# Adding the experts' output rows in DRAM by accumulating scatters, with the final norm beside the last expert, in a two-layer decoder trunk

## The chip, the cores and the metric

The kernel is one program on one core of a Trainium2 chip. The metric is the device time of one execution in microseconds (us). A core has the engines TensorE (PE in the profile, with PEld for its weight loads), VectorE (DVE), ScalarE (ACT), GpSimd (POOL) and SyncE (SP), and 16 DMA engines that all queues share.

## The reference, cut to what matters

512 tokens of width 1024 pass two layers. Layer 0 mixes tokens by a gated MLP and memory attention, layer 1 by dilated attention and memory attention. After each mixer comes a layer norm, and then a mixture of 16 experts of which each token uses two:

```python
x = layer_norm(ALPHA * x + att, ln1_g[layer], ln1_b[layer])
h = x.reshape(B * S, D)
expert, gate = route(h, w_router, b_router)          # two experts a token
ffn = moe_ffn(h, expert, gate, w_gate[layer], w_up[layer], w_down[layer])
x = layer_norm(ALPHA * x + ffn, ln2_g[layer], ln2_b[layer])
# in moe_ffn, for each expert's block of 128 rows:
return (jax.nn.silu(xblk @ w_gate[e]) * (xblk @ w_up[e])) @ w_down[e]
```

All arrays are float32.

## The kernel before, in words

`trunk` (L1422) runs `layer_a`, `moe(0)`, `layer_b`, `moe(1)` and a last block that ends layer 1.

**Experts.** `stream` (L1193) goes through the 16 experts one after the other. An expert has one block of 128 slots; a token that uses it has a rank among its tokens, and that is its slot (1024 slots are used over 16 experts, 64 of 128 in the mean). Its weights (12.6 MB) come as six halves of 2 MB through a ring of eight 2 MB slots (`load_half`, L1092): as soon as half n is used up, half n+8 is loaded into its place by SP. `block` (L1134) works in 24 chunks c of two matmuls by 128x512: c 0-3 and 4-7 are the first halves of gate and up, 8-11 and 12-15 the second halves, 16-19 and 20-23 the two halves of the down product. To keep float32 precision with fast matmuls, each weight chunk is split into a high and a low part in float32r: ACT copies the high part four chunks ahead, DVE subtracts the low part three chunks ahead (`get`, L1253; the profile's `wh` and `wl`), and `products` (L1125) makes three matmuls of each one (`mm3`, L121). The engines PE, ACT and DVE take their instructions in the order in which the program writes them (`InOrder`, L59); `jobs` hangs small work at the end of a chunk: the slot-to-token index of expert e+2, the gather of its rows (`gather`, L1075, an indirect DMA of POOL from `hbuf`), the transposes of the next rows.

**Adding up.** ACT copies the down product out of PSUM into a tile `y`, and `scatter` (L1080, an indirect DMA of POOL) writes its rows to `ybuf`, which has two rows for each token, so that no row is written twice; the scatters are declared free of each other, and unused slots are skipped because their index lies beyond the bounds. `ybuf` starts as zeros: POOL writes them in `layer_a` (L352, five DMAs of 1 MB with the copy `zbuf`), and `layer_b` writes them again for layer 1 (L555). `hbuf` holds the experts' input rows; `store` (L813) writes it after the first norm, tile by tile.

**The end of a layer.** While the last expert runs, `tail_slot` (L1290) loads the second norm's weights, reads two pairs of 128-token tiles from `hbuf` (SP), and adds the two rows of `ybuf` to each with accumulating DMAs of POOL (L1311). The last expert's rows are not scattered: a one-hot matrix `oT` brings them to their tokens by matmuls (`last_slots`, L1313). `combine` (L1384) then does, for each of the four tiles, identity matmul plus one-hot matmuls into PSUM (`z`), statistics on DVE, the normalising copy on ACT; in layer 1 `rest` (L1432) multiplies and adds the norm's weights on POOL or DVE and stores the tile by SP.

**Index.** `rows` (L1055) turns the sums of a small matmul into two indices, for `hbuf` and for `ybuf`.

## Time and profile before

| | us |
|---|---|
| median of 3 runs (1672.14 to 1672.54) | 1672.16 |
| the profiled execution, its own time | 1676.11 |
| its span, first to last instruction | 1674.4 |
| busy in the span: PE / DVE / ACT / POOL | 1582.7 / 1388.4 / 1130.7 / 181.6 |
| moved by DMA | 496.39 MB |

The profile is of one execution. Its starts are in us from the span's start. The profiled execution lies 3.95 us above the median of the runs, of which 1.7 us are outside the span.

### The profile page before, as it was taken

To read this page: it belongs to the slowest core of one execution; us is meant where nothing else is said; L and a number is where in the kernel's file an instruction comes from. 1 tells how busy PE (TensorE), PEld (TensorE's weight loads), DVE (VectorE), ACT (ScalarE), POOL (GpSimd) and SP (SyncE) were. 2 spreads that over 40 slices of the span, in tenths; PEclk is the share of its full clock that TensorE was granted. 3 is DMA by queue.
4 is the path that set the end of the run, shared out by engine and by line. 5 is a ranking of instruction groups with operands and counts; after the bars stand their busy time and mean duration, and the time that the engine had idled before them with its cause. 6 is when DMAs were issued, how large, how long until landed. Compare 5 with 4: busy or idle time off the path is not lost. (4 is left out here: it accounts for less than half of the span.)

```text
span 1674.4 us, 21460 instructions
## 1 busy us (share of the span) xinstructions
PE 1582.7 (95%) x7608; PEld 1278.8 (76%) x7608; DVE 1388.4 (83%) x1936; ACT 1130.7 (68%) x1443; POOL 181.6 (11%) x149
## 2 busy tenths in 40 slices
PE   7999889999999999999699998599999999999995
PEld 5778668888888888887587786488888888888883
DVE  3856789999999999997735556799999999999997
ACT  3544458888888888886324434288888888888882
POOL 1201400000000000001400000200000000000012
PEclk9999979999999999999799997699999999999998
DMA  8516579999999999988631151699999999999974
GB/s 347 220 51 252 202 283 378 362 380 381 370 377 365 383 380 378 373 339 243 239 123 57 64 227 32 226 362 378 379 371 365 380 373 381 380 367 381 376 233 101
DMA packets 53125, 496.39 MB, mean 296 GB/s; under 512 B 10117, under 2 KB 10245, under 8 KB 24272
## 3 DMA queue, kind: packets, MB, share of 16 engines
q1 hardware_dynamic: 39344, 449.44, 68.9%
q0 software_dynamic: 13088, 43.39, 8.1%
q10 hardware_dynamic: 576, 2.10, 0.3%
q8 instruction: 62, 1.02, 0.2%
q14 instruction: 55, 0.45, 0.1%
HBM read 479.86 MB, written 34.64 MB: 307 GB/s over the span
## 5 line engine op out<-in xcount | busy, mean ns | idle before, releaser
L68 DVE TENSOR_TENSOR wl<-wexp,wh 128x1024 fp32r<-128x1024 f32 x768 | 918.4, 1220 | 43.3 <-ACT wh L68 8.9
L68 ACT ACTIVATE wh<-wexp 128x1024 fp32r<-128x1024 f32 x762 | 797.6, 1059 | 133.7 <-PE pg L68 58.7
L68 PE MATMUL pd<-wh,ah 128*128 128x512 f32 x512 | 209.6, 409 | 0.0
L68 PE MATMUL pg<-wh,xh 128*128 128x512 f32 x512 | 204.6, 400 | 1.3 <-ACT xh L68 1.3
L68 PE MATMUL pd<-wl,ah 128*128 128x512 f32 x512 | 202.7, 396 | 0.0
L68 PE MATMUL pu<-wh,xh 128*128 128x512 f32 x512 | 202.4, 395 | 0.0
L68 PE MATMUL pd<-wh,al 128*128 128x512 f32 x512 | 202.1, 395 | 0.0
L68 PE MATMUL pg<-wl,xh 128*128 128x512 f32 x512 | 200.9, 392 | 0.0
L68 PE MATMUL pg<-wh,xl 128*128 128x512 f32 x512 | 200.8, 392 | 0.0
L68 PE MATMUL pu<-wl,xh 128*128 128x512 f32 x512 | 199.7, 390 | 0.0
L68 PE MATMUL pu<-wh,xl 128*128 128x512 f32 x512 | 199.2, 389 | 0.0
L68 PEld LDWEIGHTS pd<-wl,ah 128*128 128x128 f32 x512 | 96.1, 188 | 22.9
L68 PEld LDWEIGHTS pg<-wl,xh 128*128 128x128 f32 x512 | 96.9, 189 | 21.0
L68 PEld LDWEIGHTS pg<-wh,xh 128*128 128x128 f32 x512 | 96.9, 189 | 20.9 <-ACT xh L68 1.9
L68 PEld LDWEIGHTS pg<-wh,xl 128*128 128x128 f32 x512 | 97.1, 190 | 20.2 <-DVE xl L68 0.9
L68 PEld LDWEIGHTS pd<-wh,al 128*128 128x128 f32 x512 | 96.5, 188 | 20.0 <-DVE al L68 0.4
L68 PEld LDWEIGHTS pu<-wl,xh 128*128 128x128 f32 x512 | 96.1, 188 | 20.4
L68 PEld LDWEIGHTS pd<-wh,ah 128*128 128x128 f32 x512 | 96.3, 188 | 18.9
L68 PEld LDWEIGHTS pu<-wh,xl 128*128 128x128 f32 x512 | 96.2, 188 | 19.0
L68 PEld LDWEIGHTS pu<-wh,xh 128*128 128x128 f32 x512 | 96.1, 188 | 18.8
L1077 POOL DMA_INDIRECT xg<-hbuf,ix x32 | 42.0, 1312 | 580.5 <-PE pu L68 467.1
L1081 POOL DMA_INDIRECT ybuf<-y,ix x30 | 38.6, 1285 | 449.4 <-ACT y L68 449.4
(369 smaller groups left out, 2248.1 us busy)
## 6 DMA issues: line engine op xcount, KB each, us to landing
wexp<-w_moe SPq DMA_DIRECT2D x177, 2048.0 KB, 9.1
wexp<-w_moe SPq DMA_DIRECT2D x24, 1024.0 KB, 8.0
yrows<-ybuf POOLq DMA_DIRECT2D x8, 1024.0 KB, 9.8
wb<-wbr SPq DMA_DIRECT2D x4, 2048.0 KB, 10.6
wexp<-w_moe POOLq DMA_DIRECT2D x3, 2048.0 KB, 10.5
ybuf<-mematt POOLq DMA_DIRECT2D x4, 1024.0 KB, 14.3
wina<-wina SPq DMA_DIRECT2D x2, 2048.0 KB, 19.3
wouta<-w_out_a SPq DMA_DIRECT2D x2, 2048.0 KB, 10.9
```

The source lines that it names most:

```text
L68: r = getattr(self.eng, name)(*args, **kw)
L1077: return self.nc.gpsimd.indirect_dma_start(out=xg, out_offset=None, in_=self.hbuf, in_offset=off, bounds_check=S - 1, oob_is_err=False)
L1081: st = self.nc.gpsimd.indirect_dma_start(out=self.ybuf, out_offset=bass.IndirectOffsetOnAxis(ap=ix[:, 1], axis=0), in_=y, in_offset=None, ...
```

## The change

One DRAM buffer `sbuf` of 512 + 128 rows takes the place of `ybuf` and `zbuf`. `store` writes the norm's rows to `hbuf` and to `sbuf`; each scatter adds its 128 rows to `sbuf` in DRAM (`compute_op=OP.add`), unused slots to the 128 spare rows. The scatters are no longer declared free of each other. Layer 0 still ends in `combine`, reading `sbuf` in place of `hbuf` and `ybuf`. In layer 1 `combine` goes away. Beside the last expert, all 512 rows of `sbuf` are loaded, normalised by DVE and written by `put`, an indirect DMA by token index, whose index skips the tokens that the last expert works on; those are gathered in slot order, get the down product added, are normalised and written by one more `put`. The down product of that expert is one float32 matmul on the unsplit weights in place of three float32r ones. The gather of the first two experts now skips unused slots.

```diff
-        self.ybuf = tc.dram_tile([2 * S, D], F32, name="ybuf")
+        self.sbuf = tc.dram_tile([S + P, D], F32, name="sbuf")
         self.xbuf = tc.dram_tile([S, D], F32, name="xbuf")
-        self.zbuf = tc.dram_tile([2 * P, D], F32, name="zbuf")
...
-            for rows in [self.ybuf[2 * t * P:2 * (t + 1) * P] for t in range(NT)] + [self.zbuf]:
-                nc.gpsimd.dma_start(rows.rearrange("(p k) d -> p (k d)", k=2), zero)
+            nc.gpsimd.dma_start(self.sbuf[S:], zero[:, :D])
...
-            for t in range(NT):
-                nc.gpsimd.dma_start(self.ybuf[2 * t * P:2 * (t + 1) * P], self.zbuf)
...
-        def store(t):
-            nc.sync.dma_start(self.hbuf[t * P:(t + 1) * P, :], xr[:, t])
+        def store(*tiles):
+
+            for buf in (self.hbuf, self.sbuf):
+                for t in tiles:
+                    nc.sync.dma_start(buf[t * P:(t + 1) * P, :], xr[:, t])
...
         def between():
             for t in late:
                 rows(t)
-                store(t)
+            store(*late)
...
-        nc.vector.tensor_scalar(self.info[:, :, :, 0], o12[:, :, 1], self.p2, None, op0=OP.add)
...
-        self.dve.tensor_scalar(ix[:, 1], f, float(SKIP), None, op0=OP.add)
-        if mask:
-            return self.dve.tensor_scalar(ix[:, 0], ix[:, 1], 1, mask, op0=OP.arith_shift_right, op1=OP.bitwise_and)
-        return self.dve.tensor_scalar(ix[:, 0], ix[:, 1], 1, None, op0=OP.arith_shift_right)
+        return self.dve.tensor_scalar(ix, f, float(SKIP), self.free, op0=OP.add, op1=OP.min)
...
-    def scatter(self, y, ix, nodep):
-        st = self.nc.gpsimd.indirect_dma_start(out=self.ybuf, out_offset=bass.IndirectOffsetOnAxis(ap=ix[:, 1], axis=0),
-                                               in_=y, in_offset=None, bounds_check=2 * S - 1, oob_is_err=False)
-        for other in nodep:
-            self.tc.declare_no_dep(st.ins, other.ins, reason="rows of other tokens")
-        nodep.append(st)
+    def scatter(self, y, ix):
+
+        self.nc.gpsimd.indirect_dma_start(out=self.sbuf, out_offset=bass.IndirectOffsetOnAxis(ap=ix, axis=0),
+                                          in_=y, in_offset=None, bounds_check=S + P - 1, compute_op=OP.add)
...
-        self.dve.tensor_sub(parts[1][:, s], x3, parts[0][:, s].bitcast(F32))
+        if len(parts) > 1:
+            self.dve.tensor_sub(parts[1][:, s], x3, parts[0][:, s].bitcast(F32))
...
-        h, l = part
         for q in range(2):
             kt = 2 * j + q
             c = slice(q * 512, (q + 1) * 512)
+            if len(a) == 1:
+                self.pe.matmul(bank, a[0][:, kt], part[:, c], start=(kt == 0), stop=(kt == 7))
+                continue
+            h, l = part
             self.mm3(bank, (a[0][:, kt], a[1][:, kt]), (h[:, c], l[:, c]), start=(kt == 0), stop=(kt == 7),
                      order=((0, 0), (1, 0), (0, 1)))
...
+        final = layer == 1
+        split = 24 * NE - 8 * final
...
+            elif not final:
+                spread((11, 12, 13), self.last_slots(pool))
             else:
-                spread((11, 12, 13), self.last_slots(pool))
+                whole = [self.y_tile().rearrange("p (k n) -> p k n", k=KT)]
+                bg = self.norm_rest(pool)
+                do(0, lambda: next(bg))
+                for s in range(12, 24):
+                    do(s, lambda: next(bg, None))
...
-                while len(his) < min(k + AHEAD_H + 1, 24 * NE):
+                while len(his) < min(k + AHEAD_H + 1, split):
                     his.append(self.wh_tile())
                     self.hi = self.act.activation(his[-1], chunk(len(his) - 1), AF.Copy)
-                while len(los) < min(k + AHEAD_L + 1, 24 * NE):
+                while len(los) < min(k + AHEAD_L + 1, split):
                     n = len(los)
                     los.append(self.wl_tile(pool))
                     self.sub = self.dve.tensor_sub(los[n], chunk(n), his[n].bitcast(F32))
-                return his[k], los[k]
+                return (his[k], los[k]) if k < split else chunk(k)
...
-                        self.tail_slot(layer, n - 6 * NE)
+                        (self.final_slot if final else self.tail_slot)(layer, n - 6 * NE)
 
             def y(half, bank, e=e, last=last):
                 s = slice(half * 512, (half + 1) * 512)
+                if last and final:
+                    self.norm_slots(pool, half, bank)
+                    return
...
-                    self.scatter(ys.pop(e), self.at[e], scat)
+                    self.scatter(ys.pop(e), self.at[e])
 
             ys = {}
-            self.block(pool, xs[e], lambda e=e: fac[e], get, y, at)
+            self.block(pool, xs[e], lambda e=e: fac[e], get, y, at, whole if last and final else None)
...
-            nc.sync.dma_start(v[:, :, 0], self.hbuf[r].rearrange("(t p) d -> p t d", p=P))
+            nc.sync.dma_start(v[:, :, 0], self.sbuf[r].rearrange("(t p) d -> p t d", p=P))
+
+    def final_slot(self, layer, i):
+
+        nc = self.nc
+        if i == 0:
+            self.hgb = self.slot("ln2")
             for k in range(2):
-                rows = self.ybuf[2 * r.start:2 * r.stop].rearrange("(t p k) d -> p t k d", p=P, k=2)
-                nc.gpsimd.dma_start(v[:, :, 0], rows[:, :, k], accum_op=OP.add)
+                self.load_ln2(layer, k)
+        elif i == 2:
+            self.ts = self.slot("trows").rearrange("p (t d) -> p t d", t=NT)
+            src = self.sbuf[:S].rearrange("(t p) d -> p t d", p=P)
+            for r in (slice(0, 2), slice(2, 4)):
+                nc.sync.dma_start(self.ts[:, r], src[:, r])
+
+    def scale_rows(self, z, mean, rs):
+        self.dve.scalar_tensor_tensor(z, z, mean, self.hgb[:, :D], op0=OP.subtract, op1=OP.mult)
+        self.dve.scalar_tensor_tensor(z, z, rs, self.hgb[:, D:2 * D], op0=OP.mult, op1=OP.add)
+
+    def put(self, ix, z):
+        self.nc.gpsimd.indirect_dma_start(out=self.out, out_offset=bass.IndirectOffsetOnAxis(ap=ix, axis=0),
+                                          in_=z, in_offset=None, bounds_check=S - 1, oob_is_err=False)
+
+    def norm_rest(self, pool):
+
+        nc, dve = self.nc, self.dve
+        self.gather(self.at[NE - 1], self.xg[0], self.sbuf)
+        ix = self.keep("oix", [P, NT], I32)
+        st = self.keep("ost", [P, NT, 2, 6])
+        mv = self.keep("omv", [P, NT, 2])
+        q = self.keep("orq", [P, 3, NT])
+        nc.gpsimd.iota(ix, pattern=[[P, NT]], base=0, channel_multiplier=1)
+        yield
+        rank = self.rk[:, :, NE - 1]
+        dve.tensor_scalar(q[:, 0], rank, P + 0.5, float(SKIP), op0=OP.is_lt, op1=OP.mult)
+        dve.scalar_tensor_tensor(q[:, 0], rank, 0.5, q[:, 0], op0=OP.is_gt, op1=OP.mult)
+        dve.tensor_tensor(ix, ix, q[:, 0], op=OP.add)
+        for t in range(NT):
+            for half in range(2):
+                dve.bn_stats(st[:, t, half], self.ts[:, t, half * 512:(half + 1) * 512])
+            dve.bn_aggr(mv[:, t], st[:, t])
+            yield
+        for _ in self.rsqrt_steps(q, mv[:, :, 1], dve, EPS / ALPHA ** 2):
+            pass
+        yield
+        for t in range(NT):
+            self.scale_rows(self.ts[:, t], mv[:, t, 0:1], q[:, 0, t:t + 1])
+            self.put(ix[:, t:t + 1], self.ts[:, t])
+            yield
...
+    def norm_slots(self, pool, half, bank):
+
+        dve, z = self.dve, self.xg[0]
+        s = slice(half * 512, (half + 1) * 512)
+        if half == 0:
+            self.sst = self.keep("sst", [P, 3, 6])
+        dve.tensor_tensor(z[:, s], z[:, s], bank, op=OP.add)
+        dve.bn_stats(self.sst[:, half], z[:, s])
+        if half:
+            mv, q = self.sst[:, 2, 0:2], self.keep("srq", [P, 3, 1])
+            dve.bn_aggr(mv, self.sst[:, 0:2])
+            for _ in self.rsqrt_steps(q, mv[:, 1:2], dve, EPS / ALPHA ** 2):
+                pass
+            self.scale_rows(z, mv[:, 0:1], q[:, 0])
+            self.put(self.at[NE - 1], z)
...
-    with tc.tile_pool(name="comb", bufs=1) as pool:
-        def rest(t, zn, o):
-            n = D if t < 2 else 512
-            eng = k.eng["v" if t > 1 else "p"]
-            for i in range(0, D, n):
-                s = slice(i, i + n)
-                yield eng.tensor_mul(o[:, s], zn[:, s], k.hgb[:, s])
-                yield eng.tensor_add(o[:, s], o[:, s], k.hgb[:, D + i:D + i + n])
-                tc.nc.sync.dma_start(out[t * P:(t + 1) * P, s], o[:, s])
-
-        k.in_order("v")
-        k.combine(pool, rest, "s0 s1 b0 s2 c0 r0 b1 s3 b2 c1+c2 r1 b3 c3 r2 r3")
```

## Rows read from the trace of the kernel before

**Rows 1.** Windows, one expert: us, five engines' busy, PEclk, DMA share, GB/s.
```profile
1400.00:1435.00 35.00, 35.00 (x165) 28.63 (x165) 33.10 (x36) 28.83 (x33) 2.63 (x2) 1.00 0.97 382
```
**Rows 2.** Windows at the start of the program.
```profile
24.00:28.00 4.00, 3.07 (x7) 2.48 (x8) 2.10 (x2) 1.06 (x1) 0.00 (x0) 0.61 1.02 434
```
**Rows 3.** Timeline of POOL at the start: start, us, instruction [idle before <-releaser].
```profile
4.30 2.38 POOL L353 DMA_DIRECT2D ybuf<-mematt  x4 [0.32 <-POOL mematt L351]
```
**Rows 4.** Timeline of ACT at the start.
```profile
21.43 1.06 ACT L118 ACTIVATE xh<-xraw 128x1024 fp32r<-128x1024 f32 x1 [6.34 <-DMA xraw<-xT]
```
**Rows 5.** Timeline of PE at the start: the first projection.
```profile
19.56 0.39 PE L123 MATMUL gv<-wh,xh 128*128 128x512 f32 x1
...
20.01 0.39 PE L123 MATMUL gv<-wh,xl 128*128 128x512 f32 x1
23.48 0.50 PE L123 MATMUL gv<-wh,xh 128*128 128x512 f32 x1 [3.08 <-ACT wh L118]
...
37.29 0.28 PE L123 MATMUL gv<-wh,xh 128*128 128x256 f32 x1
```
**Rows 6.** Timelines of PE and DVE at the end of layer 0.
```profile
789.50 0.40 PE L68 MATMUL pd<-wl,ah 128*128 128x512 f32 x1
793.90 3.78 PE L68 MATMUL z<-yrows,ident 128*128 128x512 f32 x4 [4.00 <-DMA yrows<-ybuf]
...
798.57 0.70 DVE L68 BATCH_NORM_STATS2 bnst<-z 128x6 f32<-128x512 f32 x1 [1.78 <-PE z L68]
```
**Rows 7.** Timelines of PE and DVE at the end of layer 1.
```profile
1633.44 0.39 PE L68 MATMUL pd<-wh,ah 128*128 128x512 f32 x1
...
1645.13 1.88 PE L68 MATMUL z<-yrows,ident 128*128 128x512 f32 x4
...
1647.78 1.88 PE L68 MATMUL z<-yrows,ident 128*128 128x512 f32 x4
...
1647.52 1.30 DVE L68 BATCH_NORM_STATS2 bnst<-z 128x6 f32<-128x512 f32 x2 [0.86 <-PE z L68]
```
**Rows 8.** Timeline of SP at the end, and the output tensor's landings.
```profile
1657.68 13.90 SPq L1439 DMA_DIRECT2D out_dram<-yrows  x6
...
DMA to landing us min/median/max: 2.0/2.1/2.6
```
**Rows 9.** Timeline of DVE in the last expert, and its small norm operations.
```profile
1628.35 2.35 DVE L68 TENSOR_TENSOR wl<-wexp,wh 128x1024 fp32r<-128x1024 f32 x2
1633.64 0.75 DVE L68 SCALAR_TENSOR_TENSOR sg<-sg,fac,pu 128x512 f32<-128x512 f32 x1
1649.65 1.50 DVE L68 SCALAR_TENSOR_TENSOR bnmv<-bnmv 128x1 f32<-128x1 f32 x7
```
**Rows 10.** The chain at layer 1's first norm: a scaling of 128x1024 in SBUF.
```profile
1059.98 1.20 DVE xrows L811
```
**Rows 11.** POOL's last scatter and an accumulate; landings of ybuf's DMAs, of first gathers.
```profile
1611.92 1.28 POOL L1081 DMA_INDIRECT ybuf<-y,ix  x1 [33.47 <-ACT y L68]
...
1628.96 1.19 POOL L1311 DMA_DIRECT2D yrows<-ybuf  x1 [6.89 <-DMA yrows<-ybuf]
...
DMA to landing us min/median/max: 7.0/9.0/13.9
...
DMA to landing us min/median/max: 4.4/5.0/5.6
```
**Rows 12.** Windows: accumulating DMAs almost alone.
```profile
1625.00:1630.00 5.00, 5.00 (x27) 3.98 (x25) 5.00 (x6) 4.41 (x5) 1.04 (x1) 1.00 1.05 205
```
**Rows 13.** SP's last weight loads, their landings, and ACT's last splits.
```profile
1594.39 0.81 SPq L1097 DMA_DIRECT2D wexp<-w_moe  x2
...
DMA to landing us min/median/max: 7.0/8.1/9.3
...
1635.97 3.18 ACT L68 ACTIVATE wh<-wexp 128x1024 fp32r<-128x1024 f32 x3
```
**Rows 14.** SP's stores before layer 1's routing.
```profile
1061.66 7.35 SPq L814 DMA_DIRECT2D hbuf<-xrows  x3
```

More of the change, by code (lines that the diff above doesn't have):

```diff
@@ L140, in consts @@
                        allow_small_or_imprecise_dtypes=True)
-        self.p2 = c.tile([P, 1], F32, name="p2")
-        nc.gpsimd.iota(self.p2, pattern=[[0, 1]], base=0, channel_multiplier=2,
+        self.free = c.tile([P, 1], F32, name="free")
+        nc.gpsimd.iota(self.free, pattern=[[0, 1]], base=S, channel_multiplier=1,
                        allow_small_or_imprecise_dtypes=True)
         self.onesf = onesf
-        self.info = c.tile([P, NT, NE, 2], BF16, name="info")
-        nc.gpsimd.iota(self.info[:, :, :, 1], pattern=[[256, NT], [0, NE]], base=-SKIP, channel_multiplier=0,
+        self.info = c.tile([P, NT, 2], BF16, name="info")
+        nc.gpsimd.iota(self.info[:, :, 0], pattern=[[0, NT]], base=0, channel_multiplier=1,
+                       allow_small_or_imprecise_dtypes=True)
+        nc.gpsimd.iota(self.info[:, :, 1], pattern=[[P, NT]], base=-SKIP, channel_multiplier=0,
                        allow_small_or_imprecise_dtypes=True)
@@ L171, in rsqrt_steps @@
     def rsqrt_steps(self, t, var, dve, eps=EPS):
-        y, v, q = (t[:, i:i + 1] for i in range(3))
+        y, v, q = (t[:, i] if len(t.shape) > 2 else t[:, i:i + 1] for i in range(3))
         yield dve.tensor_scalar(v, var, eps, None, op0=OP.add)
@@ L178, in rsqrt_steps @@
         for three in NEWTON:
-            yield dve.scalar_tensor_tensor(q, y, v, y, op0=OP.mult, op1=OP.mult)
+            if math.prod(v.shape[1:]) == 1:
+                yield dve.scalar_tensor_tensor(q, y, v, y, op0=OP.mult, op1=OP.mult)
+            else:
+                yield dve.tensor_tensor(q, y, y, op=OP.mult)
+                yield dve.tensor_tensor(q, q, v, op=OP.mult)
             yield dve.scalar_tensor_tensor(y, q, three, y, op0=OP.subtract, op1=OP.mult)
@@ L971, in rows_index @@
         ix = self.ix[:, e]
-        self.last_index = self.slots(pool, self.rk[:, :, e:e + 1], lambda t: self.info[:, t, e], ix, None, S - 1)
+        self.last_index = self.slots(pool, self.rk[:, :, e:e + 1], lambda t: self.info[:, t], ix, None)
         self.at.append(ix)
@@ L1053, in pick, with rows, slots @@
         return v
-    def rows(self, pool, v, ix, mask=None):
+    def rows(self, pool, v, ix):
         f = pool.tile([P, 1], F32, tag="ixf", name="ixf", bufs=1)
         self.dve.tensor_reduce(f, v[:, 0:2], axis=AX.X, op=OP.add)
-        self.dve.tensor_scalar(ix[:, 1], f, float(SKIP), None, op0=OP.add)
-        if mask:
-            return self.dve.tensor_scalar(ix[:, 0], ix[:, 1], 1, mask, op0=OP.arith_shift_right, op1=OP.bitwise_and)
-        return self.dve.tensor_scalar(ix[:, 0], ix[:, 1], 1, None, op0=OP.arith_shift_right)
+        return self.dve.tensor_scalar(ix, f, float(SKIP), self.free, op0=OP.add, op1=OP.min)
     def factor(self, fac, v):
         self.dve.tensor_reduce(fac, v, axis=AX.X, op=OP.add)
-    def slots(self, pool, rank, info, ix, fac, mask=None):
+    def slots(self, pool, rank, info, ix, fac):
         v = self.pick(self.one_hot(pool, rank), info, 2 if fac is None else 5)
-        op = self.rows(pool, v, ix, mask)
+        op = self.rows(pool, v, ix)
         if fac is not None:
@@ L1130, in products, with block @@
             c = slice(q * 512, (q + 1) * 512)
+            if len(a) == 1:
+                self.pe.matmul(bank, a[0][:, kt], part[:, c], start=(kt == 0), stop=(kt == 7))
+                continue
+            h, l = part
             self.mm3(bank, (a[0][:, kt], a[1][:, kt]), (h[:, c], l[:, c]), start=(kt == 0), stop=(kt == 7),
                      order=((0, 0), (1, 0), (0, 1)))
-    def block(self, pool, x, fac, part, y, at):
+    def block(self, pool, x, fac, part, y, at, a=None):
         act, dve = self.act, self.dve
-        a = self.two(pool, ("ah", "al"))
+        a = a or self.two(pool, ("ah", "al"))
         bank, sg = {}, {}
@@ L1189, in moe, with stream @@
                 nc.scalar.activation(p[0], chunk(k), AF.Copy)
-            self.overflow(pool, layer, scat, spare)
-            self.stream(layer, px, pool, scat, loaded, chunk, parts)
-    def stream(self, layer, px, pool, scat, loaded, chunk, parts):
+            self.overflow(pool, layer, spare)
+            self.stream(layer, px, pool, loaded, chunk, parts)
+    def stream(self, layer, px, pool, loaded, chunk, parts):
         nc, tc = self.nc, self.tc
@@ L1321, in last_slots, with overflow @@
         self.act.activation(self.oT, x, AF.Copy)
-    def overflow(self, pool, layer, scat, spare):
+    def overflow(self, pool, layer, spare):
         nc, tc = self.nc, self.tc
@@ L1345, in of_block @@
                     return k2[:, :, 0]
-                nc.vector.tensor_scalar(inf[:, :, 0], of_block(self.o12[:, :, 1]), self.p2, None, op0=OP.add)
-                nc.vector.tensor_copy(inf[:, :, 1], self.info[:, :, 0, 1])
+                nc.vector.tensor_copy(inf[:, :, 0:2], self.info)
                 self.parts(inf, of_block(self.gate), k2[:, :, 1])
-                ix, fac = pool.tile([P, 2, 1], I32, name="ofx"), pool.tile([P, 1], F32, name="off")
+                ix, fac = pool.tile([P, 1], I32, name="ofx"), pool.tile([P, 1], F32, name="off")
                 self.slots(pool, rk, lambda t: inf[:, t], ix, fac)
@@ L1376, in overflow @@
                 self.block(pool, x, lambda: fac, part, y, lambda c: None)
-                self.scatter(xg, ix, scat)
+                self.scatter(xg, ix)
                 sh = pool.tile([P, 2, 8], F32, tag="ofs", name="ofs")
```

12 lines of the change are left out of this document (6 added, 6 removed).

## The prediction

> **What bounds the kernel now.** I read four views, in this order. The windows of single experts first: in a stretch of 35.0 us, the length of one expert, PE is busy for all of it at the full granted clock (1.00, that is 2.4 GHz), DVE for 33.1 us, and the DMA engines for 97% [rows 1]. Thirty-two experts of 35 us are two thirds of the span; there only PE's work counts, as long as the weights arrive. So I looked next for the stretches where PE does not work: the waits, then the timelines there. There are three that the change touches. At the **start**, PE stops at 20.2 us, resumes at 23.48 and works for some us partly at the lower of its two clocks (0.61 granted in the mean of four us, between 1.2 and 2.4 GHz) [rows 2, 5], because ACT sits 6.34 us until a piece of the input lands [rows 4], while the DMA engines are full (102%) at 434 GB/s [rows 2]. At the **end of layer 0**, PE has done the last down product at 789.73 and waits 4.00 us until `ybuf` has been added to the tiles; DVE's first statistics come at 798.57 [rows 6]. At the **end of layer 1**, the last down product ends at 1645.13 [rows 7], and 29.3 us follow to the end of the span at 1674.4, a chain of DVE work over four tiles with stores until 1671.6 [rows 8].
>
> **Start.** Removed: five DMAs of zeros, 5.24 MB, which POOL issues from 4.30 us on [rows 3], into the middle of the first loads; 0.52 MB for the spare rows stay. At 434 GB/s the 4.7 MB are 10.9 us of all DMA engines. The piece that landed at 21.4 [rows 4] is the last but one of the first 4.2 MB; without the zeros the 4.2 MB, the 0.5 MB of spare rows with them, take 10.8 us from about 3 us on, so it should land near 14. PE then needs no stop: at 20.24, 48 of the 96 matmuls of this projection are done, and the other 48, at the spacing of 0.225 just before, take 10.8 us and end at 31.1 in place of 37.3 [rows 5]. I take **-6.1 us**. Everything behind it follows PE, so it is not given back by a later load that I can see. Bounds: 0 if the pieces are late for another reason, -7 if the first pieces come earlier too.
>
> **Layer 0's end.** Removed: four accumulating DMAs of POOL. Two plain reads of `sbuf` replace them; they wait for the scatter of the expert before, which layer 1 shows issued 33 us before the down product's end (1611.92 [rows 11]), so they are back long before PE needs them. Layer 1 shows the same step without a late DMA: 2.39 us from the last down product to the first statistics (1645.13 to 1647.52 [rows 7]); layer 0 takes 8.84 [rows 6]. The bounds are -4.0, the wait alone, and -6.4, the whole difference; I take **-5.9 us**, nearer the second, because the step is the same code in both layers and PE also restarts slowly after the wait (3.78 us for four passes that take 1.88 in layer 1 [rows 6, 7]). The four copies of `zbuf` to `ybuf` in layer 1's start go too; no wait names them as its cause on the path, so 0.
>
> **Experts' stream.** PE's work is unchanged, so I cost it at 0, covered by the lead of the weight loads. What changes is the DMA work: a scatter moved 64 rows on average (0.26 MB, 0.7 us at the stream's 382 GB/s), now 128 rows (0.52 MB) that must be read, added and written. No row shows an accumulate into DRAM. The nearest is the accumulate into SBUF: 205 GB/s at 105% busy [rows 12], 195 GB/s for full engines, so 2.7 us. An expert then needs 33.9 - 0.7 + 2.7 = 35.9 us of DMA in 35.0. A deficit of 0.9 us an expert adds up to 14 us over a layer. The lead is larger: the last loads were issued at 1594.4 to 1595.2 and landed within 9.3 us, by 1604.5, and the last splits of that half begin at 1635.97 [rows 13], 31 us later. Bounds: 0 below; above see the third rival. POOL's scatter now waits for the one before it, issued 35 us earlier, and only the next gather is queued behind it: 0. One index operation less an expert on DVE, which has 1.9 us to spare: 0.
>
> **Routing.** Each layer stores four more tiles of 0.5 MB. SP's three stores of layer 1 [rows 14] are preceded in the queue by up to 1.5 MB of copies, about 4 us at the stream's rate; the first gather needs the last `hbuf` tile, which has some 8 us. Against that, the first gathers read half the rows. I take **+0.5 us** together, from -1 to +2.
>
> **Last expert of layer 1.** PE: the down product took 11.7 us with its transposes (1633.44 to 1645.13 [rows 7]). The float32 price comes from `z`: a tile (1645.13 to 1647.78) is four passes for two float32 matmuls and four float32r matmuls at 0.24 (11.7 over 48), so a pass is (2.65 - 0.96) / 4 = 0.42 and a float32 matmul 0.84 us; 16 of them are 13.5 us, 1.8 more. That is not what ends last, DVE is. The scatter before is issued at 1611.92; it lands 7 us later now [rows 11], 9 to 11 with the add; the 2 MB of rows land by about 1630. DVE is done with the splits at about 1629.0 (the pair at 1628.35 [rows 9], less the one-hot in front). Then come, in its order: three mask operations, 0.6; statistics of four tiles, each two of at most 0.65 [rows 7] and one small, 5.8; the product of gate and up, 0.75 [rows 9], done at 1636.2, for which PE, through with its first float32 chunk at 1635.1, waits 1 us; twelve small steps of 0.2 [rows 9], 2.4; tile 0 scaled in two operations of 1.20 [rows 10], 2.4. **Tile 0 is put at 1641.0.** Two more tiles, the first half of the own rows, tile 3 and the second half with its norm (0.7 + 0.6 + 0.2 + 1.9 + 2.4) end at **1655.3**; then the last put.
>
> Here I had to choose. Five puts write one output tensor by indices, and nothing in the diff declares them free of each other, as the old scatters were. So I expect each to wait for the one before to land. A landing L has bounds: 4.4 us (gather of 0.5 MB) and 7.0 us (the quickest of the DMAs on `ybuf` in this stretch, which I read as the last scatter, beside two loads [rows 11]). I take **6.0**, nearer the scatter, because nothing else moves then. The fifth lands at 1641.0 + 5 x 6.0 = 1671.0; the last store now lands 1.2 us before the span's end [rows 8], so the end is 1672.2, **-2.2 us**, from -10.2 (L 4.4) to +2.8 (L 7.0).
>
> The quickest `ybuf` landing is 7.0 us [rows 11]. The Trainium skill (DMA: Bandwidth & Descriptors, section Anatomy of one DMA) fits a GpSimd DMA as 2.0 us plus bytes over 436 GB/s; by that, as an estimate, a put of 0.5 MB lands in 3.2 us, and the end would come at the time of the first rival or earlier. No row here is as short.
>
> **Sum.** -6.1 - 5.9 + 0.5 - 2.2 = -13.7. On the profiled execution's span that is 1660.7; that execution lies 3.95 us above the median, so on the median 1672.16 it is **1658.5 us**.
>
> **Rivals.** *The puts do not wait for each other* (0.28): then the last starts at 1655.3, lands at 1661.3, and the end is 1662.5, -11.9 in place of -2.2: **1648.8**. For it: their rows are different, so no order is needed, and the output is no tile of the pool. Against: POOL here does hold back a DMA until the earlier one on the same tile has landed (6.89 us [rows 11]).
> *The start does not gain* (0.10): the zeros share the engines, but the pieces that ACT waits for were queued behind each other anyway: 1664.6.
> *The scatters starve the stream* (0.06), the slower side: an add that costs x us of all DMA engines leaves a deficit of x - 1.8 us an expert; over 15 experts it passes the lead of 31 us at x = 3.9, and from about 4.4 it eats the gain of 13.7 (two layers). At x = 6, PE would wait 2 x (63 - 31) = 64 us: **1722**. For it: 97% busy now [rows 1]. Against: x must be half as much again as the accumulate that the rows show.
> Remaining: my forecast 0.56.
>
> **Numbers.** The likeliest is 1658.5. The range takes in the free puts at its low end and, at its high end, L = 7 (+5.0) together with a start that gives little: 1646.5 to 1666.5. About 0.2%, 3.3 us, is what a measurement of this kernel can tell from no change. Slower than that: the starved stream and a small part of the waiting puts with L near 9 (0.07). Within: both small terms failing together (0.06). Faster: 0.87.
>
> **What would show it.** Right: in the first 40 us no stop of PE after 20 us and the float32r projection done near 31; at layer 0's end 2.5 to 3 us from the last `pd` to the first `bnst`, no `accum` of POOL; experts still 35.0 us apart with PE at 100%; in the last expert POOL idle before each `put` until the one before lands. Wrong: loads of weights that land over 30 us after their issue, ACT waiting for `wexp`, DVE waiting for `trows` at 1629, or `put` after `put` without a gap.

## The result and the profile of the changed kernel

The changed kernel takes 1657.56 us (median of 4 runs, 1655.82 to 1660.41); the kernel before took 1672.35 us beside it. The ratio is 0.9908, interval 0.9889 to 0.9928: 14.8 us faster, within about 1 us of the forecast. The execution that was profiled has a span of 1658.7 us (own time 1660.41) against 1674.4, so the two traces are 15.7 us apart, 0.9 more than the medians: the profiled executions lie 2.9 and 3.8 us above the medians of their kernels. Every distance between two stages below is read within one trace.

First PE's timeline, at the places where a stage begins or ends. The changed kernel:

```profile
31.36 0.28 PE L122 MATMUL gv<-wh,xh 128*128 128x256 f32 x1
...
221.50 0.79 PE L68 MATMUL pg<-wh,xh 128*128 128x512 f32 x1 [1.49 <-ACT xh L68]
...
784.42 0.39 PE L68 MATMUL pd<-wl,ah 128*128 128x512 f32 x1
...
808.53 0.58 PE L122 MATMUL pq<-x,wh 128*128 128x256 f32 x1
...
1064.06 0.20 PE L959 MATMUL rank<-rt,before 128*128 128x16 bf16 x1 [8.90 <-DVE rt L952]
...
1073.53 0.45 PE L68 MATMUL xt<-ident,xg 128*128 128x128 f32 x1 [7.01 <-DMA xg<-hbuf,ix]
...
1625.21 0.59 PE L68 MATMUL pd<-wexp,y 128*128 128x512 f32 x1
```

The same places of the kernel before, where [rows 5 to 7] do not have them already:

```profile
227.46 0.80 PE L68 MATMUL pg<-wh,xh 128*128 128x512 f32 x1 [1.27 <-ACT xh L68]
...
819.22 0.58 PE L123 MATMUL pq<-x,wh 128*128 128x256 f32 x1
...
1073.27 0.20 PE L955 MATMUL rank<-rt,before 128*128 128x16 bf16 x1 [8.90 <-DVE rt L947]
...
1082.15 0.48 PE L68 MATMUL xt<-ident,xg 128*128 128x128 f32 x1 [6.42 <-DMA xg<-hbuf,ix]
```

Read as pairs, these rows say how far the changed kernel is ahead at each place, and the steps between them what each stage gave:

| stage, to the row | ahead by, us | the stage gave | forecast |
|---|---|---|---|
| start, to 31.36 | 5.9 | -5.9 | -6.1 |
| layer 0's router and mixer, to 221.50 | 6.0 | 0 | part of +0.5 |
| experts of layer 0, to 784.42 | 5.1 | +0.9 | 0 |
| layer 0's end, to 808.53 | 10.7 | -5.6 | -5.9 |
| layer 1's mixer, to 1064.06 | 9.2 | +1.5 | 0 |
| layer 1's routing, to 1073.53 | 8.6 | +0.6 | part of +0.5 |
| experts of layer 1, to 1625.21 (1633.44 before [rows 7]) | 8.2 | +0.4 | 0 |
| last expert's down product to the end of the span | 15.7 | -7.5 | -2.2 |

The table is of one trace of each kernel. Other traces of the same code differ by up to 1.4 us at layer 0's end and by some 4 us in layer 1's mixer, as shown below, so these two rows are known no better than that.

**Start.** PE doesn't stop after 20 us any more, the DMA engines are no longer full in the window of [rows 2] (84%), and ACT's wait of 6.34 us [rows 4] is one of 1.65. Windows, then ACT's timeline, of the changed kernel:

```profile
24.00:28.00 4.00, 4.00 (x20) 3.30 (x19) 0.69 (x1) 1.87 (x2) 0.48 (x1) 1.00 0.84 341
```
```profile
14.74 1.06 ACT L117 ACTIVATE xh<-xraw 128x1024 fp32r<-128x1024 f32 x1 [1.65 <-DMA xraw<-xT]
```

**Layer 0's end.** The wait for `ybuf` [rows 6] is gone, but another took part of its place. Timelines of PE, POOL and DVE in the changed kernel:

```profile
784.65 1.88 PE L68 MATMUL z<-yrows,ident 128*128 128x512 f32 x4
785.97 1.26 PE L68 MATMUL z<-ylast 128*128 128x512 f32 x3
790.15 0.54 PE L68 MATMUL z<-ylast 128*128 128x512 f32 x1 [2.93 <-DVE ylast L68]
...
786.82 2.33 POOL L118 TENSOR_TENSOR wl<-wb,wh 128x1024 fp32r<-128x1024 f32 x1
...
786.88 2.36 DVE L466 TENSOR_SCALAR rel_i<-rel_i 128x129 int32<-128x129 int32 x1 [5.18 <-POOL rel_i L465]
...
789.42 0.68 DVE L68 TENSOR_TENSOR ylast<-pd,ylast 128x512 fp32r<-128x512 f32 x1
...
790.21 1.29 DVE L68 BATCH_NORM_STATS2 bnst<-z 128x6 f32<-128x512 f32 x2
```

PE waits 2.93 us for the split of `ylast`, which stands behind a small integer operation on `rel_i` (`bias_tiles`, part of the next layer's mixer). That operation takes 2.36 us, as long as POOL's weight split beside it. In the kernel before it took 0.23 us, behind the `ylast` split; there its successor met POOL's split, behind the first statistics (DVE's and POOL's timelines of the kernel before):

```profile
800.03 2.49 DVE L464 CAST rel<-rel_i 128x129 f32<-128x129 int32 x1
```
```profile
800.04 2.39 POOL L119 TENSOR_TENSOR wl<-wb,wh 128x1024 fp32r<-128x1024 f32 x1
```

The program's text is the same there. What changed is the order: without the accumulating DMAs in front POOL builds `rel_i` at once, and DVE's queue has the operation ahead of the last `ylast` split.

**The end.** POOL's five puts, DVE's last operation, and the landings of the output tensor's DMAs:

```profile
1633.01 1.82 POOL L1341 DMA_INDIRECT out_dram<-trows,oix  x1 [20.62 <-DVE trows L68]
1637.91 0.99 POOL L1341 DMA_INDIRECT out_dram<-trows,oix  x1 [3.08 <-DVE trows L68]
1641.91 0.98 POOL L1341 DMA_INDIRECT out_dram<-trows,oix  x1 [3.01 <-DVE trows L68]
1645.99 1.12 POOL L1341 DMA_INDIRECT out_dram<-trows,oix  x1 [3.11 <-DMA out_dram<-trows,oix]
1651.16 0.98 POOL L1341 DMA_INDIRECT out_dram<-xg,ix  x1 [4.05 <-issue]
...
1646.30 1.28 DVE L68 SCALAR_TENSOR_TENSOR xg<-xg,srq,ln 128x1024 f32<-128x1024 f32 x1
```
```profile
DMA to landing us min/median/max: 3.2/3.3/4.1
```

The puts are 4.0 to 5.2 us apart although DVE has rows ready: DVE is done at 1647.58, and the last put goes out at 1651.16. The landings, counted from the start of the issue, are 4.1, 3.2, 3.3, 3.5 and 3.2 us in this order, so that each put goes out 0.8 us, the last one 1.7 us, after the one before has landed. The rows of 1637.91 and 1641.91 name DVE as what ended the wait, but it had long been done with these tiles (with the first of them at 1635.24). After the last put 7.5 us pass to the end of the span.

**Stream.** DMA queues over six experts, 470 to 680 us (packets, MB, share of the 16 engines; then landings). Before:

```profile
q0 software_dynamic: 1728, 3.23, 4.0%
...
wexp<-w_moe SPq DMA_DIRECT2D x36, 2048.0 KB, 8.6
ybuf<-y,ix POOLq DMA_INDIRECT x6, 9.6
```

The changed kernel:

```profile
q1 hardware_dynamic: 5179, 75.42, 89.7%
q0 software_dynamic: 1728, 4.71, 9.5%
...
wexp<-w_moe SPq DMA_DIRECT2D x36, 2048.0 KB, 10.6
sbuf<-y,ix POOLq DMA_INDIRECT x6, 14.4
```

The software queue (one gather and one scatter an expert) takes 3.3 us an expert in place of 1.4, and the engines are 99.5% busy. The weights land 2 us later and nobody waits for them.

### The profile page after: what moved, and what is told of

Its sections match the earlier page's. It is cut to its first block, busy times and chain, and to the rows that moved or that the text cites. A ratio compares the mean times of both kernels' runs of the same rounds, so it can differ in the third digit from the quotient of the medians.

```text
span 1658.7 us, 21243 instructions
## 1 busy us (share of the span) xinstructions
PE 1575.5 (95%) x7556; PEld 1270.9 (77%) x7556; DVE 1375.0 (83%) x1880; ACT 1115.6 (67%) x1424; POOL 184.1 (11%) x137
## 5 line engine op out<-in xcount | busy, mean ns | idle before, releaser
L68 ACT ACTIVATE wh<-wexp 128x1024 fp32r<-128x1024 f32 x754 | 789.1, 1059 | 134.5 <-PE pg L68 59.5
L68 PE MATMUL pd<-wh,ah 128*128 128x512 f32 x496 | 203.0, 409 | 0.0
L68 PE MATMUL pd<-wh,al 128*128 128x512 f32 x496 | 197.8, 399 | 0.0
L68 PE MATMUL pd<-wl,ah 128*128 128x512 f32 x496 | 194.8, 393 | 0.0
L68 PEld LDWEIGHTS pu<-wl,xh 128*128 128x128 f32 x512 | 96.1, 188 | 20.4
L1083 POOL DMA_INDIRECT sbuf<-y,ix x30 | 56.2, 1873 | 452.3 <-ACT y L68 452.3
## 6 DMA issues: line engine op xcount, KB each, us to landing
wexp<-w_moe SPq DMA_DIRECT2D x177, 2048.0 KB, 10.4
```

The costliest lines, as they stand in the source:

```text
L68: r = getattr(self.eng, name)(*args, **kw)
L1083: self.nc.gpsimd.indirect_dma_start(out=self.sbuf, out_offset=bass.IndirectOffsetOnAxis(ap=ix, axis=0), in_=y, in_offset=None, bounds_chec ...
```

## The experiments

All but one are edits of the changed kernel. Their ratios are to runs of the kernel before on the same chip; where an effect is smaller than the intervals, the trace decides.

### Zeros back at the start

```diff
+        self.ybuf = tc.dram_tile([2 * S, D], F32, name="ybuf")
...
+            for rows in [self.ybuf[2 * t * P:2 * (t + 1) * P] for t in range(NT)]:
+                nc.gpsimd.dma_start(rows.rearrange("(p k) d -> p (k d)", k=2), zero)
             nc.gpsimd.dma_start(self.sbuf[S:], zero[:, :D])
```

> The changed kernel with the four 1 MB writes of zeros put back at the start (into a buffer that nothing reads). My theory, that these bytes delay the input pieces ACT waits for: PE stops again in the first projection, whose last matmul moves from 31.4 us back to about 37, the changed kernel's time goes up by 5 to 6 us (1657.6 to about 1663), and nothing later takes it back. Rival, that the bytes are hidden and the start gained from something else: the projection still ends within 1 us of 31.4 and the time does not move.

1664.50 us, ratio 0.9934 (0.9915 to 0.9953). ACT's wait and PE's stop are back; the matmul that stood at 31.36 stands at 36.91, and the span is 6.0 us longer. ACT's and PE's timelines:

```profile
21.10 1.06 ACT L118 ACTIVATE xh<-xraw 128x1024 fp32r<-128x1024 f32 x1 [6.36 <-DMA xraw<-xT]
```
```profile
23.16 0.51 PE L123 MATMUL gv<-wh,xh 128*128 128x512 f32 x1 [3.25 <-ACT wh L118]
...
36.91 0.28 PE L123 MATMUL gv<-wh,xh 128*128 128x256 f32 x1
```

So the bytes of the zeros are what the start had lost its time to, and the rival that it gains nothing falls.

### The kernel before with its zeros written later

```diff
-            for rows in [self.ybuf[2 * t * P:2 * (t + 1) * P] for t in range(NT)] + [self.zbuf]:
-                nc.gpsimd.dma_start(rows.rearrange("(p k) d -> p (k d)", k=2), zero)
+            nc.gpsimd.dma_start(self.zbuf.rearrange("(p k) d -> p (k d)", k=2), zero)
...
+        with tc.issue_after(self.sub.ins):
+            for t in range(NT):
+                nc.gpsimd.dma_start(self.ybuf[2 * t * P:2 * (t + 1) * P], self.zbuf)
```

> The kernel before with four of its five writes of zeros moved from the start behind POOL's work of the first layer's mixer (as copies of zbuf); nothing else moves. My theory of the start, from the other side: PE no longer stops after 20 us, the first projection ends at 31 to 32 us in place of 37.3, and the kernel before becomes 5 to 6 us faster (ratio about 0.9967). Rival: the copies cost later what they free at the start, time as before. Beside it, the pace of PE: the 32 experts of the changed kernel took 0.16% longer each with no wait in them; if that is the chip or the execution and not the change, this kernel on this chip shows 35.05 us an expert too, and if it is the change, 35.00.

1667.25 us, ratio 0.9971 (0.9960 to 0.9982). The matmul of 37.29 [rows 5] comes at 31.40:

```profile
31.40 0.28 PE L123 MATMUL gv<-wh,xh 128*128 128x256 f32 x1
```

By the medians 5.4 us, a third of the change's gain, is thus to be had by moving one loop. On the pace of PE: from expert 0's first `at` transposes to expert 15's last, in layer 0, this kernel needs 536.39 us, like the kernel before (536.39); the changed kernel and each variant of it that was profiled, on three chips, need 537.2 to 537.3. It is the program and not the chip, and as the scatters without the add show below, not the add.

### The accumulating DMAs back at layer 0's end

The kernel with the zeros at the start, and in `tail_slot`:

```diff
             nc.sync.dma_start(v[:, :, 0], self.sbuf[r].rearrange("(t p) d -> p t d", p=P))
+            for k in range(2):
+                rows = self.ybuf[2 * r.start:2 * r.stop].rearrange("(t p k) d -> p t k d", p=P, k=2)
+                nc.gpsimd.dma_start(v[:, :, 0], rows[:, :, k], accum_op=OP.add)
```

> The kernel with the zeros put back, and at the end of layer 0 the four accumulating DMAs of POOL as well; they add those zeros. My theory, that the wait for them is what layer 0's end gained: PE waits about 4 us for yrows after the last down product, and against the kernel with the zeros alone the time goes up by 5.6 us (about 1669), with no change before 750 us. Rival, that the gain came from the smaller scatters and the plain reads being early: PE waits under 1 us and the difference is under 1.5 us.

1672.83 us, ratio 0.9993 (0.9981 to 1.0006), 8.3 us above the kernel with the zeros alone by the medians and 5.8 by the spans. PE, from its timeline, waits longer than the 4.0 us of [rows 6]:

```profile
798.38 3.78 PE L68 MATMUL z<-yrows,ident 128*128 128x512 f32 x4 [7.64 <-DMA yrows<-ybuf]
```

From the last down product to the first `pq` it takes 30.5 us against 24.1 with the zeros alone. By the medians, undoing both, the start and layer 0's end, gives back nearly all of the change's 14.8 us. The trace shows that the gain of the last expert is still there (32.8 us from the first matmul of its last down product to the end of the span, 41.0 in the kernel before); about half of it is eaten by some 4 us that this kernel loses elsewhere, as in layer 1's routing (10.2 us from `rank` to the transposes in place of 8.9). The rest is seen in the spans alone (1670.5 against 1674.4), since the profiled execution of the kernel before lies 3.8 us above its median.

### Puts free of each other

```diff
+        self.puts = []
...
+        for other in self.puts:
+            self.tc.declare_no_dep(st.ins, other.ins, reason="rows of other tokens")
+        self.puts.append(st)
```

> The changed kernel with the five puts declared free of each other. My theory, that only the order put on them makes the last one wait: puts leave POOL as soon as DVE has the rows, the last at about 1647.6 on the changed kernel's clock in place of 1651.2, and the time falls by 3.5 us (1657.6 to about 1654). Rival, that the queue behind POOL takes one indirect DMA at a time anyway, or that the end is set by something after the last put: the last landing and the time stay where they are, within 1 us.

1654.23 us, ratio 0.9877 (0.9857 to 0.9897). POOL's timeline:

```profile
1632.46 1.78 POOL L1342 DMA_INDIRECT out_dram<-trows,oix  x1 [0.70 <-DVE trows L68]
...
1644.99 0.98 POOL L1342 DMA_INDIRECT out_dram<-xg,ix  x1 [5.20 <-DVE xg L68]
```

The last put now waits for DVE alone (done at 1644.52) and 7.5 us follow it as before. From the last expert's `at` transposes (1624.95) to the end it is 27.55 us in place of 30.68: **-3.1 us** for the order of the puts.

### Scatters that do not add

```diff
-                                          in_=y, in_offset=None, bounds_check=S + P - 1, compute_op=OP.add)
+                                          in_=y, in_offset=None, bounds_check=S + P - 1)
```

> The changed kernel whose scatters write their rows without adding, so the sum over a token's two experts and its input row is left out (the last writer stays). My theory, that the add costs DMA time which the stream's lead hides: the software queue's share in a window of six experts falls from 9.5% to about 5%, a scatter lands after 10 to 11 us in place of 14, weights after 9 in place of 10.4, and the time stays within 1.5 us of the changed kernel's. Rival, that the adds slow PE through late weights: several us faster. A third: the 0.05 us by which an expert became longer (35.00 to 35.05) comes from the adds; then 1.6 us faster.

1659.01 us, ratio 0.9904 (0.9885 to 0.9922): no difference from the changed kernel. The queues in the window of six experts:

```profile
q0 software_dynamic: 1728, 4.71, 5.6%
...
sbuf<-y,ix POOLq DMA_INDIRECT x6, 12.1
```

The add costs 9.5 - 5.6 = 3.9% of 210 us over six, 1.4 us of all DMA engines an expert, and the stream hides it. I had expected the weights to land in 9 us; they land in 10.4, hardly earlier than with the add (10.6), so it isn't the add that made them later. An expert is as long as with the add (537.27 us over the sixteen), so the third theory falls as well.

### Every scatter twice

```diff
-                    self.scatter(ys.pop(e), self.at[e])
+                    yt = ys.pop(e)
+                    for _ in range(2):
+                        self.scatter(yt, self.at[e])
```

> The changed kernel with every scatter issued twice, so each expert's rows are counted double in the sum. In the trace of the changed kernel the software queue takes 9.5% of 210 us for six experts, 3.3 us an expert, against 1.4 before, so an accumulating scatter is about 2.6 us of all DMA engines, and the engines are 99.5% busy. My theory: with a second one an expert needs about 37.4 us of DMA in 35.0, the deficit adds up to 2.4 x 15 = 36 us in a layer against a lead of about 31, so weights land later and later and PE waits some 5 us (0 to 15) at the end of each layer: about 1668 (1657 to 1690). Rival, that the engines were starved by accumulates of another price: at 4 us each it would be 1710 and more; or the busy share counts time that queues share, and nothing changes.

1659.46 us, ratio 0.9925 (0.9913 to 0.9938): some 2 us more by the medians, less than the intervals can tell, and at the low end of what I expected. The queues over six experts, and the weights' landings in the windows 300 to 400 and 600 to 700 us:

```profile
q1 hardware_dynamic: 5133, 74.75, 84.4%
q0 software_dynamic: 2592, 7.86, 17.0%
```
```profile
wexp<-w_moe SPq DMA_DIRECT2D x17, 2048.0 KB, 12.6
...
wexp<-w_moe SPq DMA_DIRECT2D x18, 2048.0 KB, 20.2
```

The price was right: 17.0 - 9.5 = 7.5% of 210 us over six is 2.6 us for an accumulating scatter. The picture of a growing debt was right too, but not its size: the weights land later and later, 7.6 us in 300 us or 0.9 us an expert, not the 2.4 that I had summed. The reason is in the first row: the weights' share fell from 89.7% to 84.4% for 1% fewer bytes. The time that a packet of weights takes was thus not the same in the two runs, and shares of different queues could not be added up to a need. At 20 us the landings are still far inside the lead of 31, and the 16 experts take 537.25 us. What the doubled scatter costs is in the last expert, where it lands too late: the tile `y`, which takes the transposed product there, is still being read (3.94 us of ACT waiting for `sbuf`), and DVE waits for `trows`. From layer 1's first transposes to the end this run takes 589.4 us in place of 585.2; its span is no longer than the changed kernel's because layer 1's mixer, which the edit doesn't touch, took 251.3 us in place of 255.5 (see the last section). ACT's timeline:

```profile
1616.77 0.60 ACT L68 ACTIVATE y<-at 128x512 f32<-128x512 f32 x1 [3.94 <-DMA sbuf<-y,ix]
```

### hbuf first

```diff
-                            store(i)
+                            store(i, bufs=(self.hbuf,))
...
-                        store(2)
+                        store(2, bufs=(self.hbuf,))
...
-            store(*late)
+            store(*late, bufs=(self.hbuf,))
+            store(*(late if fill else range(4)), bufs=(self.sbuf,))
```

> The changed kernel in which layer 1 issues its four hbuf stores first and the four copies to sbuf behind them. My theory, that the first gather of layer 1 (issued 1068.93, 2.0 us after its index, where the kernel before needed 0.8 us) waits for an hbuf tile queued behind the copies: it is issued within 1 us of its index and everything behind it moves up by 1 to 1.5 us (1657.6 to about 1656.4). Rival, that the wait is one of POOL's own and not of the stores: no change in that step.

1657.73 us, ratio 0.9916 (0.9903 to 0.9929): a gain of 1 us, as expected, is too small for the medians to show. In the trace the first gather goes out 1.0 us after the index operations (1066.22, done at 1065.27; it was 2.0). In the changed kernel the last `hbuf` store, issued behind copies, lands after 8.6 us, at 1068.04 (after 4.7 in the kernel before), and the gather goes out at 1068.93, so it did wait for that tile. From `rank` to PE's transposes it is 8.4 us in place of 9.5, and 8.9 in the kernel before. PE's timeline:

```profile
1070.81 1.51 PE L68 MATMUL xt<-ident,xg 128*128 128x128 f32 x6 [5.99 <-DVE wl L68]
```

The row names DVE, but the transposes read only the gathered rows, whose landing has no record in this trace; at 4.3 us from the issue, as in the changed kernel, it is at 1070.5. In the run of the three repairs, with the same stores, the row names the gather.

### rel_i behind the ylast split

```diff
+        with self.tc.issue_after(self.sub.ins):
             nc.vector.tensor_scalar(mi, mi, 3, None, op0=OP.bitwise_and)
```

> The changed kernel in which DVE's first operation on rel_i, at the end of layer 0, is put behind the last split of ylast; nothing else moves. My theory, that this operation took 2.36 us instead of 0.23 because POOL was splitting a weight at the same time, and held the ylast split that PE's next matmul waits for (2.93 us): that matmul starts about 2.9 us earlier, the first statistics come 2.4 to 3 us after the last down product in place of 5.5, and the time falls by 2.5 to 3 us (1657.6 to about 1655). Rival, that the DVE is slowed whatever comes first, or that the norm's later steps wait for POOL anyway: the ylast split itself takes over 2 us, or the projection behind the norm (pq, 808.5 in the changed kernel) starts no earlier.

1659.15 us, ratio 0.9920 (0.9907 to 0.9933): no gain that can be measured. The operation took 2.38 us again, now ahead of the first statistics, which came 4.5 us after the last down product (784.72 to 789.25) in place of 5.5; the first `pq` came 22.7 us after it, not 23.9. The operation was named rightly, but the cure moved it by one place only. Hence the next.

### rel behind the whole norm

```diff
+        with self.tc.issue_after(self.eng["v"].prev):
             nc.vector.tensor_scalar(mi, mi, 3, None, op0=OP.bitwise_and)
```

> The changed kernel with DVE's four operations on rel_i and rel put behind the whole norm at the end of layer 0. Putting the first of them behind the ylast split alone made PE's next tile 3.1 us earlier but gave 1.2 us at the first pq and 0.5 later, because the same operation still took 2.38 us beside POOL's weight split, now ahead of the first statistics. My theory: with all four out of the way the first statistics come 2.2 to 2.6 us after the last down product (5.5 in the changed kernel), the first pq at 21 us after it (23.9), and the time falls by 2 to 3 us. Rival, that the chain behind the norm (POOL's two multiplications, the transposes of tile 1) sets the pace: the first pq moves by 1.2 us at most.

1654.75 us, ratio 0.9888 (0.9871 to 0.9904). DVE's timeline, then POOL's:

```profile
786.77 0.69 DVE L68 TENSOR_TENSOR ylast<-pd,ylast 128x512 fp32r<-128x512 f32 x1 [4.54 <-ACT ylast L68]
787.62 1.30 DVE L68 BATCH_NORM_STATS2 bnst<-z 128x6 f32<-128x512 f32 x2 [0.15 <-PE z L68]
...
789.19 0.53 DVE L68 TENSOR_SCALAR bnmv<-bnmv 128x1 f32<-128x1 f32 x3
...
820.97 0.21 DVE L467 TENSOR_SCALAR rel_i<-rel_i 128x129 int32<-128x129 int32 x1
```
```profile
787.36 2.35 POOL L118 TENSOR_TENSOR wl<-wb,wh 128x1024 fp32r<-128x1024 f32 x1
```

The first statistics come 2.4 us after the last down product (785.18), the 2.39 that the kernel before shows in layer 1; the operation on `rel_i` takes 0.21 us where POOL is idle; the first `pq` comes 20.4 us after the last down product instead of 23.9. That is **-3.5 us**, a little more than the 2 to 3 that I had expected. The span shows 6.3 less; the rest lies in layer 1's mixer (251.2 us in place of 255.5) and is not the edit's, as the run of the three repairs, which has it too, needs 255.4 there; see the last section.

### The last down product split again

```diff
-        split = 24 * NE - 8 * final
+        split = 24 * NE
...
-                whole = [self.y_tile().rearrange("p (k n) -> p k n", k=KT)]
...
-            self.block(pool, xs[e], lambda e=e: fac[e], get, y, at, whole if last and final else None)
+            self.block(pool, xs[e], lambda e=e: fac[e], get, y, at)
```

> The changed kernel with one part undone: the last expert's down product again as three float32r matmuls on split weights. My theory, that in the last expert DVE ends last and the float32 product is worth its PE time because it takes eight splits of 1.2 us and two of 0.7 from DVE: DVE's last operation comes 10 to 11 us later, the last put no longer waits for the one before (it waited 3.1 us longer than its rows), and the time rises by 7 to 8 us (1657.6 to about 1665). Rival, that the float32 product is the cost, because a matmul takes 0.86 us in place of three of 0.235: the time falls by 1 to 2 us.

1668.09 us, ratio 0.9964 (0.9950 to 0.9978); the span is 7.6 us longer. Timelines of DVE and POOL:

```profile
1655.84 1.28 DVE L68 SCALAR_TENSOR_TENSOR xg<-xg,srq,ln 128x1024 f32<-128x1024 f32 x1
...
1658.80 0.99 POOL L1340 DMA_INDIRECT out_dram<-xg,ix  x1 [4.04 <-issue]
```

DVE ends at 1657.12, 9.5 us later, and the last put goes out 7.6 later. I had expected that it would no longer wait for the put before it; it still does, 1.7 us behind its rows (3.6 in the changed kernel), so the end hangs on DVE and on the chain of puts together. The float32 product, which costs PE more, is worth as much as the whole gain of the last expert (7.5).

### The three repairs together

> The changed kernel with free puts (measured -3.1 us in the trace), layer 1's hbuf stores ahead of the copies (gather issued 1.2 us after its index in place of 2.0, and PE not waiting for rows that are late), and the four rel operations behind the norm. If the three gains add up: 3.1 + 0.8 to 1.2 + 2 to 3, so 5.9 to 7.3 us under the changed kernel, 1650 to 1652, ratio to the kernel before 0.987. If the later ones are taken back by other waits, about 1654 as with the free puts alone.

1652.63 us, ratio 0.9863 (0.9844 to 0.9883), the best of all: 4.9 us under the changed kernel by the medians, where the forecast had 5.9 to 7.3, and 7.5 by the ratios, each to the kernel before on the same chip. `rank` to transposes 8.7 us, last down product to first `pq` 20.4, last put on DVE's heels (DVE done at 1643.18):

```profile
1643.64 0.99 POOL L1344 DMA_INDIRECT out_dram<-xg,ix  x1 [5.20 <-DVE xg L68]
```

The steps add up to 3.1 + 0.8 + 3.5 = 7.4 us by the traces; the span shows 7.5.

## Why the prediction was right, and where it was not

**Start: right**, size and mechanism (-6.1 forecast, -5.9 found, 5.6 to 6 both ways in two experiments).

**Layer 0's end: right in sum, wrong in its parts.** I took the size from layer 1's step, "because the step is the same code in both layers", and named 2.5 to 3 us from the last `pd` to the first statistics as the sign. They came after 5.6 us (784.65 to 790.21): at this point only 3.3 of the 5.9 us were there, below my lower bound of 4.0, and the other 2.3 came behind it, where I had forecast nothing. That the sum fits is luck. The step that failed is that I named nothing as late next: POOL, set free, builds `rel_i` sooner, and DVE's operation on it, which now met POOL's weight split in front of the critical `ylast` split, took 2.36 us in place of 0.23. That held back 3.5 us. With `rel` out of the way the statistics come after 2.4 us, as read from layer 1, and -9.1 is there (first `pq` 29.5 us behind the last down product before, 20.4 then). The rows were there to see: in the kernel before POOL's work on `rel` follows at once on its waits for `yrows`, and one of DVE's operations on it already took 2.49 us.

So not all of the 9.1 is the wait for `ybuf`: the kernel before lost time to a meeting of its own, behind the statistics. In the trace of the kernel before with late zeros, whose code is the same here, that operation meets nothing, and the step takes 28.1 us:

```profile
793.15 0.21 DVE L466 CAST rel<-rel_i 128x129 f32<-128x129 int32 x1
```

Held against that trace, the change gave 4.2 us here, and 7.7 with `rel` moved.

**Stream: right.** I estimated 2.7 us of DMA an accumulating scatter from an accumulate into SBUF; doubled scatters give 2.6. That the lead of 31 us hides it is shown by the scatters without the add. The rival that they starve the stream was rightly held small: even two of them do not. Its working, though, adds shares, and with doubled scatters the debt grew at less than half of what such a sum says (0.9 us an expert, not 2.4).

**Routing: right**, size and mechanism: +0.5 forecast, +0.6 found. The copies that I put at about 4 us delay the last `hbuf` store by 3.9 (8.6 us to land in place of 4.7); 0.8 to 1.0 are to be had by another order of the stores.

**Last expert: the mechanism was right, two terms were mis-sized.** In before's clock, less the 8.2 us by which this stretch is early, I had tile 0 put at 1632.8 (1633.01 found), and DVE done at 1647.1 (1647.58). The puts do wait for each other, as forecast. But I took 6.0 us for each, "nearer the scatter". They go out 4.5 us apart in the mean (18.15 over four), next to my lower bound of 4.4, and land in 3.2 to 4.1. From the first put to the last landing that makes 21.4 us in place of 30.0. The other way, 7.5 us pass from the last put's issue to the end of the span, 4.3 more than its landing of 3.2, where I had put 1.2; what fills them no row shows. So the gain was 7.5 us and not 2.2. The fit of the Trainium skill (DMA: Bandwidth & Descriptors, section Anatomy of one DMA), 3.2 us by estimate for 0.5 MB, is close to what the landings show; I had set it aside because no row was as short.

**The first rival** (free puts) had the wrong price for the same reason: freeing the puts is worth 3.1 us, not 9.7.

**What I left out** cost 2.8 us in this pair of traces: the slightly longer experts (+0.9 and +0.4) and layer 1's mixer (+1.5). Whether the second is the change's is not shown: the mixer took 251.2 to 255.7 us in the changed kernel and its variants, 254.1 and 252.6 in the kernel before and its variant. These 2.8 us took back half of the 5.3 that the end gained beyond the forecast, and the medians are 0.9 us closer than the traces. That 1658.5 lies so close to 1657.56 is in part luck; the sum was better than its terms.

## What to carry to other kernels

When a wait is taken from one engine, list what that engine's queue holds next and which instructions of other engines will meet it: here 3.5 of 9.1 us at layer 0's end went to an operation that moved in front of the critical one when POOL was no longer held up. Where several DMAs write one tensor by disjoint indices, say so, and price the chain they form without it as count times the landing of a quiet transfer and what passes until the next goes out (0.8 to 1.7 us here), not by the landing of a loaded one. And in a stretch where DVE ends last, an operation that is dearer on PE but needs no splits is a gain, here about 8 us.

## What the runs showed of the hardware that I had not expected

- A small DVE operation on SBUF operands (128x129 int32) takes 0.21 to 0.23 us alone and 2.36 to 2.38 us when it starts behind a POOL operation of 2.33 to 2.35 us. The statistics on PSUM, beside the same POOL operation in the run with `rel` behind the norm, keep their time (1.30 us for two). The Trainium skill (SBUF — State Buffer, section Who interferes with whom) says that DVE's `tensor_scalar` can enter a mode in which it and GpSimd take one pair of ports in turn, and that whoever issues second is blocked for the whole of the other's instruction. The rows above agree: the DVE operation ended 0.09 us after POOL's. Not every `tensor_scalar` was held, though: the first of the three on 128x1 that started at 789.19 in the run with `rel` behind the norm, 0.5 us before POOL's end, was not (0.53 us for the three).
- An accumulating scatter of 128 rows of 4 KB into DRAM takes 2.6 us of all DMA engines, of which the add is 1.4, and 1.87 us of POOL to issue (1.30 in the run whose scatters do not add).
- In 40 us of layer 1's mixer, from some 74 to 34 us before `rank`, the mean granted clock was 0.86 in the kernel before (1000 to 1040 us), 0.82 in the changed kernel (990 to 1030), and 0.94 in the run with `rel` behind the norm (983 to 1023) and in the one with doubled scatters (986 to 1026): stretches of PE at the lower of its two levels come and go there, with the same 1210 matmuls in the same order in all four. From the first `pq` to `rank` these took 254.1, 255.5, 251.2 and 251.3 us. Why the stretches differ stays open.
- The changed program's matmuls follow each other 0.16% more slowly over whole experts (35.05 us in place of 35.00), with no wait in any row, in all its variants. Neither the chip nor the add is the cause; what is stays open.
